# A diffusion block on one core: the first modulation as four column strips, one ring of weights, another layout for the merge

## The chip, the cores and the metric

The kernel runs on one core of a Trainium2 chip. The metric is device time in microseconds (us) of one execution. The kernel before took 1096.97 us, the median of three runs from 1096.02 to 1098.99. Engines are named as in the profile: PE is TensorE (PEld its weight loads), DVE VectorE, ACT ScalarE, POOL GpSimd, SP SyncE, which here only issues transfers.

## The reference

One layer of a diffusion transformer works on 512 latent tokens and 256 context tokens of width 1024, in float32. What matters for the change:

```
m_lat = (silu(c) @ mod_w + mod_b)            # six sections of 1024: sh1, sc1, g1, sh2, sc2, g2
m_ctx = silu(c_ctx) @ mod_w + mod_b
h_lat = rms_norm(x, g) * (1 + sc1) + sh1
h_ctx = rms_norm(ctx, g) * (1 + csc1) + csh1
... h @ w_in -> two token mixers (gated DeltaNet, HGRN2), gates g_a, g_b, m_a, m_b
ya = gated_head_norm(oa, g_a) @ w_up_a ;  yb = gated_head_norm(ob, g_b) @ w_up_b
x = x + g1 * ((sigmoid(m_a) * ya + sigmoid(m_b) * yb) @ w_out)
x = x + g2 * swiglu(rms_norm(x, g') * (1 + sc2) + sh2)
```

So the first two sections of `mod_w` (1024 by 2048 numbers) are needed for two vectors, the latent one and the context one, before the first projection can begin.

## The kernel before

Every large product is made in three parts of reduced-precision float32 (fp32r): each operand is split into a high part, `hi`, and the rest, `lo`, and hi·hi, hi·lo and lo·hi are summed in PSUM (`mm3`, L105). `split` (L92 to L97) loads a tile of weights on SP's queue, makes `hi` on ACT and `lo` on DVE; its buffers, two of each kind, are a ring named `ring["w"]`. All tiles are taken from pools that lie on top of each other in SBUF; a tile that comes to lie on an older one waits for that one's last use. The order of the instructions on each engine is set by a list scheduler from the order of the program and a priority, `tc.cur_priority`; stages of the two mixers are interleaved by the written plan `PLAN`.

The first stage runs so. `load_x` loads the tokens, `load_mod(d)` for each of eight blocks d of 128 output columns a tile `mw` with all 1024 rows of `mod_w` for a shift and a scale block, `wr` the raw weights of six gates. `modulation(d, s)` (L264, L266, L270) multiplies, on DVE, each of the eight 128-row parts of `mw` by its 128 numbers of the vector s (0 latent, 1 context) and adds them up in two accumulators `macc`; then PE sums over the partitions by four matmuls with a column of ones into `pmod0`. `mod_columns` (L275 to L277) adds the biases and multiplies by the norm's weights; the result, `mcol`, has a column for each feature block. `normed` transposes the tokens of block d on PE (L283, `px`), applies `mcol` twice on ACT (`hhi` L285 or `chi` for the context, and a float32 twin L287), and takes the low part on DVE (L288). `prepare(d)` does that for the latent tokens and splits `wr`. The loop over d then issues 18 matmuls (L316, `pg`) into six banks, after which two more gates (`gate`, `pgate`) are computed. Between them the context's eight modulations are issued, behind them the context's `normed`, and then the small projection `pab` (L369), with `abT` (L370), on which the DeltaNet's gates depend. The main stage follows: HGRN heads (`h_...`) and DeltaNet pairs (`g_...`, `p_...`), with gates in the gaps and further sections of the modulation on DVE (`mwe`, `mwb`; L111 sums their columns on four strips of the array, `column_sums`).

Late in that stage the first pool of the left side, `wp`, belongs to the stack `early` and is given up with it; a second ring, `wf`, was opened on the right side (after L911) and serves the remaining gates and everything behind them: the merge (`branch`, `up`, matmuls `pup`), the output projection (`pwo`) and the SwiGLU (`pf`, `pfo`). The merge's pool `mg` (its outputs `mh`, `ml`) lies below `yp` (the gated branch outputs `yh`, `yl`, the gates read back `ug`, `mg`, the branch outputs `uy`, and the product `us`).

Of the kernel before, what the change touches and what calls it, by code (L numbers as in the profile page):

```python
# [7 lines left out]
F32 = mybir.dt.float32  # L8
# [40 lines left out]
def body(tc, T, out, tap=None):  # L49
# [8 lines left out]
    with ExitStack() as root:  # L58
        def pool(name, bufs=1, side=None, **kw):
            return tc.tile_pool(name=name, bufs=bufs, side=side, reuse_waits="tile", **kw)  # L60

        cp = root.enter_context(pool("cp"))
        hpool = root.enter_context(pool("hpool"))
        early = ExitStack()
        ring = {"w": early.enter_context(pool("wp", 2))}
# [13 lines left out]
        def pmm(name):  # L79
            return bank("mm", name)  # L80
# [73 lines left out]
        with ExitStack() as st:  # L154
# [32 lines left out]
            def load_mod(d):  # L187
                mw = s1.tile([P, KT, 256], F32, name=f"mw{d}")
                for j in range(2):
                    nc.sync.dma_start(mw[:, :, P * j:P * j + P],  # L190
                                      T["mod_w"][0, :, D * j + P * d:D * j + P * d + P].rearrange("(k p) f -> p k f", p=P))
                mws.append(mw)

            load_mod(0)
            for g in (2, 3, 4, 5):
                load_x(g)
            for d in range(KT):
                if d > 0:
                    load_mod(d)
                wr = s1.tile([P, NG0 * P], F32, name=f"wr{d}", tag="wr", bufs=3)  # L200
                nc.sync.dma_start(wr[:, :], W_IN[P * d:P * d + P, C_MB:C_MB + NG0 * P])
                wraws.append(wr)
# [39 lines left out]

            ss = s1.tile([P, 6], F32, name="ss")
# [14 lines left out]
            def modulation(d, s):  # L258

                accs = [sp.tile([P, 256], F32, name=f"macc{d}_{s}{i}", tag=f"macc{i}", bufs=4) for i in range(2)]  # L260
                for k in range(KT):
                    acc, col = accs[k % 2], sc[:, 8 * s + k:8 * s + k + 1]
                    if k < 2:
                        nc.vector.tensor_scalar_mul(acc[:, :], mws[d][:, k, :], col)  # L264
                    else:
                        nc.vector.scalar_tensor_tensor(acc[:, :], mws[d][:, k, :], col, acc[:, :], op0=ALU.mult, op1=ALU.add)  # L266
                for j in range(2):
                    c = 16 * s + 2 * d + j
                    for i, acc in enumerate(accs):
                        nc.tensor.matmul(pmod0[:, c:c + 1], acc[:, P * j:P * j + P], ones[:, 0:1], start=(i == 0), stop=(i == 1))  # L270

            def mod_columns(s, d0, d1):

                ps = pmod0[:, 16 * s + 2 * d0:16 * s + 2 * d1].rearrange("p (d j) -> p d j", j=2)
                nc.vector.tensor_tensor(mcol[:, s, d0:d1, 0], ps[:, :, 0], mb_sh[:, d0:d1], op=ALU.add)  # L275
                nc.vector.tensor_tensor(mcol[:, s, d0:d1, 1], ps[:, :, 1], mb1[:, d0:d1], op=ALU.add)
                nc.vector.tensor_tensor(mcol[:, s, d0:d1, 1], mcol[:, s, d0:d1, 1], g_mix[:, d0:d1], op=ALU.mult)  # L277
# [13 lines left out]
            pmod0 = bank("ha", "pmod0")  # L291
# [11 lines left out]
            modulation(0, 0)  # L303
            mod_columns(0, 0, 1)
            prepare(0)
            modulation(1, 0)
            for d in range(KT):
                if d + 2 < KT:
                    modulation(d + 2, 0)
                if d + 1 < KT:  # L310
                    mod_columns(0, d + 1, d + 2)
                    prepare(d + 1)
                wh, wl = wparts[d]
                for n, (u, v) in enumerate(((wh, hhi), (wl, hhi), (wh, hlo))):
                    for i in range(NG0):
                        nc.tensor.matmul(pg0[i][:, :], u[:, P * i:P * i + P], v[:, d, :],  # L316
                                         start=(d == 0 and n == 0), stop=(d == KT - 1 and n == 2))
            for i in range(NG0):
                gate_out(16 + i, pg0[i], sp, "gt")
            norm_rows((0, 1))  # L320
            cd = list(range(KT))
# [5 lines left out]
            for d in cd:  # L327
                modulation(d, 1)
            mod_columns(1, 0, KT)
# [584 lines left out]
        wf = root.enter_context(pool("wf", 2, side="right"))  # L914
# [7 lines left out]
        ring["mod"] = md.enter_context(pool("md", side="right"))  # L922
        mods += [mod_quarter(*q) for q in quarters]
        here = tc.cur_priority
        tc.cur_priority = here + 5000
        while gates or mods:
            if gates:
                gate(gates.pop(0), ring["mod"], wf, "ga")
            mod_steps(6)
# [5 lines left out]
        early.close()  # L935
        tc.cur_priority = here + 5000 + 10000
        ring["w"] = wf

        with pool("mg", 1) as mg:
            mh = mg.tile([P, KT, SEQ], F32R, name="mh")  # L940
            ml = mg.tile([P, KT, SEQ], F32R, name="ml")
            mt = view(x1, 0, ((SEQ, KT), (1, SEQ)))
            with pool("yp", 1) as yp:
                def branch(br):

                    yh = yp.tile([P, NH, SEQ], F32R, name=f"yh{br}", tag="yh", bufs=2)
                    yl = yp.tile([P, NH, SEQ], F32R, name=f"yl{br}", tag="yl", bufs=2)
                    for h in range(NH):
                        gt = yp.tile([P, SEQ], F32, name=f"ug{br}{h}", tag="ug", bufs=4)
                        nc.sync.dma_start(gt[:, :], gdram[4 * br + h, :, :])  # L950
                        sg = yp.tile([P, SEQ], F32, name=f"us{br}{h}", tag="us", bufs=2)
                        nc.scalar.activation(gt[:, :], gt[:, :], AF.Silu)
                        yt = yp.tile([P, SEQ], F32, name=f"uy{br}{h}", tag="uy", bufs=3)
                        nc.sync.dma_start(yt[:, :], ydram[4 * br + h, :, :])
                        nc.vector.tensor_tensor(sg[:, :], gt[:, :], yt[:, :], op=ALU.mult)
                        nc.scalar.copy(yh[:, h, :], sg[:, :])
                        nc.vector.tensor_tensor(yl[:, h, :], sg[:, :], yh[:, h, :].bitcast(F32), op=ALU.subtract)
                    return yh, yl

                def up(br, W, ys):  # L960

                    for j in range(0, KT, 2):
                        w = split([W[:, P * j:P * j + 2 * P]], 4, 2 * P)
                        for i in (j, j + 1):
                            ps = pmm(f"pup{br}{i}")
                            o = P * (i - j)
                            mm3(ps[:, :], [lambda k, t=t: t[:, k, o:o + P] for t in w], [lambda k, t=t: t[:, k, :] for t in ys], 4)
                            gt = yp.tile([P, SEQ], F32, name=f"mg{br}{i}", tag="ug", bufs=4)
                            nc.sync.dma_start(gt[:, :], gdram[8 + 8 * br + i, :, :])
                            nc.scalar.activation(gt[:, :], gt[:, :], AF.Sigmoid)  # L970
                            if br == 0:
                                nc.vector.tensor_tensor(mt[:, i, :], gt[:, :], ps[:, :], op=ALU.mult)
                            else:
                                nc.vector.tensor_tensor(gt[:, :], gt[:, :], ps[:, :], op=ALU.mult)
                                nc.vector.tensor_tensor(gt[:, :], mt[:, i, :], gt[:, :], op=ALU.add)
                                nc.scalar.copy(mh[:, i, :], gt[:, :])
                                nc.vector.tensor_tensor(ml[:, i, :], gt[:, :], mh[:, i, :].bitcast(F32), op=ALU.subtract)
                        yield

                merge_a = up(0, T["w_up_a"][0], branch(0))  # L980
                next(merge_a)
                yb = branch(1)
                for _ in merge_a:
                    pass
                mod_sums()
                md.close()
                row_bcast(g1b, mbc[:, 16:24], "ga")
                nc.vector.scalar_tensor_tensor(A2[:, :], mbc[:, 32:40], 1.0, g_ffn, op0=ALU.add, op1=ALU.mult)
                for _ in up(1, T["w_up_b"][0], yb):
                    pass  # L990
# [134 lines left out]
```

## Time and profile before

| what | number |
|---|---|
| median of three runs | 1096.97 us |
| profiled execution, its own time | 1099.97 us |
| its span in the profile | 1098.3 us |
| mean granted clock of PE | 0.983 |
| PE busy | 1034.3 us, 94% |
| DVE busy | 699.2 us, 64% |
| ACT busy | 554.6 us, 50% |
| bytes moved | 122.06 MB, mean 111 GB/s |

The span runs from the first instruction to the last; some 1.7 us of the execution's own time lie outside it. PE counts as busy while a matmul is in its pipeline, and neighbours overlap, so the pace of matmuls is read from the chain (time of a group divided by its count), not from the mean duration of one.

### The profile page before, as it was taken

The numbers are of one execution on the slowest core, as the hardware profiler recorded it, in microseconds if no ns is written. First come the engines' busy times: TensorE is split into PE (matmuls) and PEld (weight loads), VectorE is DVE, ScalarE is ACT, GpSimd is POOL, SyncE is SP. The second block draws the span as 40 slices with busy tenths as digits, with TensorE's granted clock in tenths as the row PEclk, the third lists the DMA queues.
The fourth block names the chain that finished last, engine by engine and source line by source line (L and its number), as shares of the span: only waits on it lengthen the run. The fifth ranks groups of instructions, "written<-read, shape, count | busy, mean of one in ns | idle before, by whom it ended". The sixth has DMA issues, their size and how long they took to land.

```text
span 1098.3 us, 16604 instructions
## 1 busy us (share of the span) xinstructions
PE 1034.3 (94%) x6439; PEld 856.0 (78%) x6439; DVE 699.2 (64%) x1373; ACT 554.6 (50%) x1042; POOL 75.7 (7%) x132
## 2 busy tenths in 40 slices
PE   4999999979899999999989999999999999999996
PEld 3787788858797877789777787788888878888785
DVE  5896876789867967976796575686433333322524
ACT  3454578757877765887764743442222222221212
POOL 0010000220002022001111000110000000000000
PEclk9998999999999999999999999999999999999998
DMA  9943412122004213200728843454333323322222
GB/s 304 283 145 126 135 44 72 51 76 67 3 10 143 61 48 87 58 3 28 221 90 269 275 152 127 129 170 152 96 96 97 96 77 96 96 96 95 84 92 94
DMA packets 142721, 122.06 MB, mean 111 GB/s; under 512 B 5533, under 2 KB 118451, under 8 KB 142643
## 3 DMA queue, kind: packets, MB, share of 16 engines
q1 hardware_dynamic: 135907, 100.20, 30.0%
q0 software_dynamic: 4640, 17.30, 4.7%
q10 hardware_dynamic: 2096, 3.50, 0.9%
q8 instruction: 50, 0.82, 0.3%
q14 instruction: 28, 0.23, 0.1%
HBM read 110.51 MB, written 10.49 MB: 110 GB/s over the span
## 4 chain that ended last, share of the span: by engine, by line
PE 70%; DVE 12%; ACT 6%; issue 5%; DMA 4%; POOL 3%; SPq 0%; POOLq 0%; ACTq 0%; DVEq 0%
PE pf L105 22%; PE pfo L105 10%; PE pgate L105 5%; PE pup L105 4%; PE pg L316 3%; PE h_z L105 3%; PE pwo L105 3%; DVE lo L97 2%; PE h_zv L105 2%; PE p_s_pk L795 1%; PE pmod L270 1%; PE h_pA L482 1%; PE g_k_zl L105 1%; PE p_s_pk L786 1%; DMA mwb<-in_mod_w_dram 1%
## 5 line engine op out<-in xcount | busy, mean ns | idle before, releaser
L95 ACT CAST hi<-raw 128x1024 fp32r<-128x1024 f32 (+1 forms) x137 | 135.8, 992 | 310.1 <-PE pf L105 169.9
L97 DVE TENSOR_TENSOR lo<-raw,hi 128x1024 fp32r<-128x1024 f32 (+1 forms) x137 | 157.8, 1152 | 183.3 <-ACT hi L95 183.0
L105 PE MATMUL pf<-hhi,lo 128*128 128x512 f32 (+1 forms) x368 | 142.8, 389 | 0.4 <-DVE lo L97 0.4
L105 PE MATMUL pf<-hlo,hi 128*128 128x512 f32 (+1 forms) x368 | 142.8, 389 | 0.3 <-DVE hlo L1038 0.3
L105 PE MATMUL pf<-hhi,hi 128*128 128x512 f32 (+1 forms) x368 | 142.4, 389 | 0.0
L105 PEld LDWEIGHTS pf<-hhi,lo 128*128 128x128 f32 x368 | 70.2, 191 | 16.0 <-DVE lo L97 1.2
L105 PEld LDWEIGHTS pf<-hlo,hi 128*128 128x128 f32 x368 | 70.1, 191 | 15.3 <-DVE hlo L1038 0.5
L105 PEld LDWEIGHTS pf<-hhi,hi 128*128 128x128 f32 x368 | 69.9, 191 | 14.7
L105 PE MATMUL pfo<-lo,uh 128*128 128x512 f32 x176 | 69.8, 396 | 0.1
L105 PE MATMUL pfo<-hi,ul 128*128 128x512 f32 x176 | 69.5, 395 | 0.0
L105 PE MATMUL pfo<-hi,uh 128*128 128x512 f32 x176 | 68.7, 395 | 0.0
L105 PE MATMUL pgate<-hhi,lo 128*128 128x512 f32 x144 | 61.0, 424 | 6.2 <-DVE lo L97 6.2
L105 PE MATMUL pgate<-hhi,hi 128*128 128x512 f32 x144 | 60.5, 420 | 1.9 <-ACT hi L95 1.9
L105 PE MATMUL pgate<-hlo,hi 128*128 128x512 f32 x144 | 59.4, 413 | 0.0
L1061 DVE TENSOR_TENSOR sg<-sg,pf 128x512 f32<-128x512 f32 x22 | 15.1, 687 | 51.6 <-PE pf L105 51.5
L829 DVE SCALAR_TENSOR_TENSOR acc<-mwb,sc,acc 128x256 f32<-128x256 f32 x72 | 34.4, 482 | 10.1 <-DMA mwb<-in_mod_w_dram 8.9
L266 DVE SCALAR_TENSOR_TENSOR macc<-mw,sc,macc 128x256 f32<-128x256 f32 x96 | 39.9, 476 | 0.0
L105 PEld LDWEIGHTS pfo<-lo,uh 128*128 128x128 f32 x176 | 33.2, 188 | 8.6 <-DVE lo L97 1.0
L105 PEld LDWEIGHTS pgate<-hhi,lo 128*128 128x128 f32 x144 | 28.8, 200 | 13.8 <-DVE lo L97 8.6
L105 PEld LDWEIGHTS pfo<-hi,uh 128*128 128x128 f32 x176 | 32.9, 188 | 8.0 <-ACT hi L95 0.6
L105 PEld LDWEIGHTS pfo<-hi,ul 128*128 128x128 f32 x176 | 33.2, 188 | 7.6
L105 PE MATMUL h_z<-hhi,hi 128*128 128x512 f32 x96 | 38.1, 397 | 0.4 <-ACT abT L370 0.3
(426 smaller groups left out, 2523.0 us busy)
## 6 DMA issues: line engine op xcount, KB each, us to landing
raw<-in_ffn_w_in_dram SPq DMA_DIRECT2D x44, 512.0 KB, 3.8
raw<-in_w_in_dram SPq DMA_DIRECT2D x37, 512.0 KB, 3.9
raw<-in_ffn_w_out_dram SPq DMA_DIRECT2D x22, 512.0 KB, 3.5
mwb<-in_mod_w_dram POOLq DMA_DIRECT2D x18, 512.0 KB, 4.6
mw<-in_mod_w_dram SPq DMA_DIRECT2D x16, 512.0 KB, 6.2
mwe<-in_mod_w_dram POOLq DMA_DIRECT2D x7, 1024.0 KB, 6.2
gdram<-gt SPq DMA_DIRECT2D x24, 256.0 KB, 2.1
raw<-in_w_in_dram SPq DMA_DIRECT2D x18, 256.0 KB, 3.2
```

Of the source, the lines that this page charges most:

```text
L95: nc.scalar.copy(hi[:, :, :], raw[:, :, :])
L97: nc.vector.tensor_tensor(lo[:, :, :], raw[:, :, :], hi.bitcast(F32), op=ALU.subtract)
L105: nc.tensor.matmul(ps, a[u](k), b[v](k), start=(start and n == 0), stop=(stop and n == tot - 1))
L266: nc.vector.scalar_tensor_tensor(acc[:, :], mws[d][:, k, :], col, acc[:, :], op0=ALU.mult, op1=ALU.add)
L270: nc.tensor.matmul(pmod0[:, c:c + 1], acc[:, P * j:P * j + P], ones[:, 0:1], start=(i == 0), stop=(i == 1))
L316: nc.tensor.matmul(pg0[i][:, :], u[:, P * i:P * i + P], v[:, d, :], start=(d == 0 and n == 0), stop=(d == KT - 1 and n == 2))
L482: nc.tensor.matmul(pA[:, P * c:P * c + P], kq[:, 0, P * c:P * c + P], kq[:, 1, P * c:P * c + P], start=True, stop=True)
L786: nc.tensor.matmul(pk[:, P:2 * P], N[:, d, e, g, :], rt[:, :], start=True, stop=True)
L795: nc.tensor.matmul(pk[:, 2 * P:3 * P], kend[:, :], u[:, :], start=True, stop=True)
L829: nc.vector.scalar_tensor_tensor(acc[:, :], mw[:, k - k0, :], sc[:, k:k + 1], acc[:, :], op0=ALU.mult, op1=ALU.add)
L1061: nc.vector.tensor_tensor(sg[:, :], sg[:, :], pgu[1][:, :], op=ALU.mult)
```

## The change

Three things change.

First, the modulation. `load_mod(c)` now loads a tile of 512 rows (half of the inputs) by 512 columns (256 of the shift and 256 of the scale); six buffers serve eight such tiles, and the raw weights `wr` have five buffers instead of three. The latent tokens are loaded ahead of the first such tile. `modulation(q)`, called four times instead of sixteen, does two blocks d and both vectors at once: eight float32 matmuls, for each half of the rows one in each of the four 32-column strips of the array, with a 32-column operand `sch` that holds the two vectors and 30 columns of zeros, and 512 columns of `mod_w` streaming; each strip leaves its part of the sum on 32 partitions of one bank. DVE copies the bank to `mr`, and four matmuls with the two-column tile `comb` add the four strips and turn the result into columns; three DVE operations finish `mcol` for latent and context together. The DVE accumulation and the context's modulations between the gates are gone, and the context's row norms are issued inside the loop, at d = 6.

Second, `wp` now belongs to the root and is the ring for all stages; the gates of the late main stage get a ring of their own, `wx`, given up at the end of that stage. `wf` is gone.

Third, the merge's pools change places: `yp` is opened ahead of `mg`, its `yh`, `yl` are plain tiles, one for each branch, and the product is written into `yt` instead of a tile `sg`.

```
-            def load_mod(d):
-                mw = s1.tile([P, KT, 256], F32, name=f"mw{d}")
+            def load_mod(c):
+                mw = s1.tile([P, 4, 512], F32, name=f"mw{c}", tag="mw", bufs=6)
...
+            def modulation(q):
+                ps = bank("ha", f"pmod{q}")
+                for half in range(2):
+                    for k in range(4):
+                        nc.tensor.matmul(ps[32 * k:32 * k + 32, :], sch[:, 4 * half + k, :], mws[2 * q + half][:, k, :],
+                                         start=(half == 0), stop=(half == 1), tile_position=(0, 32 * k))
+                mr = s1.tile([P, 512], F32, name=f"mr{q}", tag="mr", bufs=2)
+                nc.vector.tensor_copy(mr[:, :], ps[:, :])
+                for i in range(4):
+                    nc.tensor.matmul(ps[:, 2 * i:2 * i + 2], mr[:, P * i:P * i + P], comb[:, :], start=True, stop=True)
...
-            modulation(0, 0)
-            mod_columns(0, 0, 1)
+            modulation(0)
             prepare(0)
-            modulation(1, 0)
             for d in range(KT):
-                if d + 2 < KT:
-                    modulation(d + 2, 0)
+                if d % 2 == 0 and d + 2 < KT:
+                    modulation(d // 2 + 1)
                 if d + 1 < KT:
-                    mod_columns(0, d + 1, d + 2)
                     prepare(d + 1)
+                if d == 6:
+                    norm_rows((0, 1))
...
             for i in rest[0:2]:
                 gate(i, sp)
-                for _ in range(8):
-                    if cd:
-                        modulation(cd.pop(0), 1)
...
-        wf = root.enter_context(pool("wf", 2, side="right"))
...
+        wx = gx.enter_context(pool("wx", 2, side="right"))
...
-        ring["w"] = wf
-        with pool("mg", 1) as mg:
+        with pool("yp", 1) as yp, pool("mg", 1) as mg:
...
-                        nc.vector.tensor_tensor(sg[:, :], gt[:, :], yt[:, :], op=ALU.mult)
+                    nc.vector.tensor_tensor(yt[:, :], gt[:, :], yt[:, :], op=ALU.mult)
```

More of the change, by code (lines that the diff above doesn't have):

```diff
@@ L63, in body @@
         hpool = root.enter_context(pool("hpool"))
+        ring = {"w": root.enter_context(pool("wp", 2))}
         early = ExitStack()
-        ring = {"w": early.enter_context(pool("wp", 2))}
         cpool = early.enter_context(pool("cpool"))
@@ L197, in body @@
             for d in range(KT):
[L198 to L202, printed above, removed]
+                load_mod(d)
+                if d % 2 == 0:
+                    continue
+                for e in (d - 1, d):
+                    wr = s1.tile([P, NG0 * P], F32, name=f"wr{e}", tag="wr", bufs=5)
+                    nc.sync.dma_start(wr[:, :], W_IN[P * e:P * e + P, C_MB:C_MB + NG0 * P])
+                    wraws.append(wr)
                 if d == 1:
@@ L241, in body @@
             nc.vector.tensor_scalar_add(mb1[:, :], mb_sc, 1.0)
+            sch = s1.tile([P, KT, 32], F32, name="sch")
+            nc.gpsimd.memset(sch[:, :, :], 0.0)
+            nc.vector.tensor_copy(sch[:, :, 0:2], sc.rearrange("p (s k) -> p k s", s=2))
+            comb = s1.tile([P, 2], F32, name="comb")
+            nc.vector.tensor_tensor(comb[:, :], ident[:, 0:2], ident[:, 32:34], op=ALU.add)
+            for j in (64, 96):
+                nc.vector.tensor_tensor(comb[:, :], comb[:, :], ident[:, j:j + 2], op=ALU.add)
             ss = s1.tile([P, 6], F32, name="ss")
@@ L256, in body @@
             mcol = s1.tile([P, 2, 8, 2], F32, name="mcol")
[L258 to L277, printed above, removed]
+            def modulation(q):
[8 more added lines that the diff above has]
+                    nc.tensor.matmul(ps[:, 2 * i:2 * i + 2], mr[:, P * i:P * i + P], comb[:, :], start=True, stop=True)
+                col = ps[:, 0:8].rearrange("p (j d s) -> p j s d", j=2, s=2)
+                dd = slice(2 * q, 2 * q + 2)
+                def both(x):
+                    return x[:, dd].unsqueeze(1).to_broadcast([P, 2, 2])
+                nc.vector.tensor_tensor(mcol[:, :, dd, 0], col[:, 0, :, :], both(mb_sh), op=ALU.add)
+                nc.vector.tensor_tensor(mcol[:, :, dd, 1], col[:, 1, :, :], both(mb1), op=ALU.add)
+                nc.vector.tensor_tensor(mcol[:, :, dd, 1], mcol[:, :, dd, 1], both(g_mix), op=ALU.mult)
@@ L290, in body @@
             norm_rows((2, 3, 4, 5))
-            pmod0 = bank("ha", "pmod0")
             pg0 = [bank(t, f"pg0_{i}") for i, t in enumerate(("mm", "mm", "ga", "ga", "ga", "fa"))]
@@ L319, in body @@
                 gate_out(16 + i, pg0[i], sp, "gt")
-            norm_rows((0, 1))
-            cd = list(range(KT))
             for i in rest[0:2]:
                 gate(i, sp)
-                for _ in range(8):
-                    if cd:
-                        modulation(cd.pop(0), 1)
-            for d in cd:
-                modulation(d, 1)
-            mod_columns(1, 0, KT)
             for d in range(KT):
@@ L922, in body @@
         ring["mod"] = md.enter_context(pool("md", side="right"))
+        gx = ExitStack()
+        wx = gx.enter_context(pool("wx", 2, side="right"))
         mods += [mod_quarter(*q) for q in quarters]
@@ L927, in body @@
             if gates:
-                gate(gates.pop(0), ring["mod"], wf, "ga")
+                gate(gates.pop(0), ring["mod"], wx, "ga")
             mod_steps(6)
@@ L940, in body @@
             mh = mg.tile([P, KT, SEQ], F32R, name="mh")
             ml = mg.tile([P, KT, SEQ], F32R, name="ml")
[L942 to L954, printed above, removed]
-                        nc.vector.tensor_tensor(sg[:, :], gt[:, :], yt[:, :], op=ALU.mult)
[L956 to L990, printed above, removed]
@@ L993, in body @@
+            merge_a = up(0, T["w_up_a"][0], branch(0))
+            next(merge_a)
+            yb = branch(1)
+            for _ in merge_a:
+                pass
+            mod_sums()
+            md.close()
+            row_bcast(g1b, mbc[:, 16:24], "ga")
+            nc.vector.scalar_tensor_tensor(A2[:, :], mbc[:, 32:40], 1.0, g_ffn, op0=ALU.add, op1=ALU.mult)
+            for _ in up(1, T["w_up_b"][0], yb):
+                pass
             with pool("xp", 2) as xp:
```

38 lines of the change are left out of this document (35 added, 3 removed).

## The prediction

> **What bounds the kernel now.** I read the page first, for the engine that fills the span.
>
> ```profile
> PE 1034.3 (94%) x6439; PEld 856.0 (78%) x6439; DVE 699.2 (64%) x1373; ACT 554.6 (50%) x1042; POOL 75.7 (7%) x132
> ...
> PE   4999999979899999999989999999999999999996
> ...
> DVE  5896876789867967976796575686433333322524
> ```
>
> TensorE (PE) is the bound almost everywhere, and VectorE (DVE) is close to it only in the first tenth. So a gain must take matmul time away, or a place where PE stands still. Next comes the chain that ended last, from the first projection matmul to the first dense stretch of the main stage.
>
> ```profile
> 19.68 1.65 PE pg L316 x3
> ...
> 60.36 7.74 PE pg L316 x34
> 68.11 5.45 PE pgate L105 x24
> 73.55 3.46 PE pmod L270 x32
> ...
> 77.59 0.54 PE px L283 x4
> ...
> 85.95 3.29 PE pmod L270 x24
> ...
> 90.82 0.57 ACT chi L285
> ...
> 97.64 1.87 PE pab L369 x10
> ...
> 99.53 0.58 ACT abT L370
> ...
> 101.78 1.35 PE h_z L105 x5
> ```
>
> Three parts are seen: the lat projection (pg) to 68.1; two gates, with the context's modulation between and behind them, to 91.4; the small a/b projection (pab) to 101.8, where the h_z matmuls of the first HGRN head become dense. Busy time of each engine in these parts, and in two late ones (DVE's, ACT's and POOL's columns follow PE's; then granted clock, DMA share, GB/s):
>
> ```profile
> 20.00:40.00 20.00, 18.16 (x83) 14.60 (x83) 16.45 (x44) 5.57 (x8) 0.00 (x0) 0.91 1.13 310
> ...
> 19.60:68.10 48.50, 46.58 (x229) 38.76 (x230) 41.82 (x114) 22.85 (x33) 1.38 (x2) 0.96 0.81 224
> 68.10:91.40 23.30, 21.13 (x120) 18.43 (x118) 20.58 (x57) 7.04 (x11) 1.94 (x2) 0.85 0.68 226
> 91.40:101.70 10.30, 9.95 (x53) 6.59 (x53) 5.04 (x16) 8.04 (x19) 0.32 (x6) 0.83 0.36 102
> 550.00:600.00 50.00, 45.25 (x243) 37.03 (x244) 40.31 (x76) 27.33 (x53) 6.53 (x8) 0.97 0.53 170
> 600.00:650.00 50.00, 49.22 (x293) 39.44 (x292) 32.03 (x48) 30.79 (x45) 0.00 (x0) 1.00 0.70 232
> ```
>
> Between 68.1 and 91.4 DVE is busy 20.6 of 23.3 us, and PE's granted clock is only 0.85: PE's "busy" there is partly slow and partly tiny matmuls that wait for DVE. What DVE does is the second half of these groups:
>
> ```profile
> L266 DVE SCALAR_TENSOR_TENSOR macc<-mw,sc,macc 128x256 f32<-128x256 f32 x96 | 39.9, 476 | 0.0
> L270 PE MATMUL pmod<-ones,macc 128*128 128x1 f32 x128 | 17.2, 252 | 6.0 <-DVE macc L266 6.0
> ...
> L264 DVE TENSOR_SCALAR macc<-mw,sc 128x256 f32<-128x256 f32 x32 | 9.9, 345 | 1.6 <-DMA mw<-in_mod_w_dram 1.6
> ```
>
> That is 49.8 us of DVE for the modulation of latent and context, one after the other.
>
> **The change part by part.**
>
> *Prices.* The code makes 64 pmod matmuls and L270 has 128 records, so a float32 matmul is two records. In the chain above, 32 records take 3.46 us, 0.108 us each. A gate matmul takes 5.45/24 = 0.227 us, a pg matmul 7.74/34 = 0.228, a px transpose 0.54/4 = 0.135. Further rows, from the chain and the timeline:
>
> ```profile
> 572.01 0.67 PE h_pS L548 x6
> ...
> 633.55 0.23 PE pmo L111 x16
> ```
> ```profile
> 289.09 0.92 PE L760 MATMUL p_pYb<-p_N,p_T 64*64 64x64 f32 x24 [0.34 <-ACT p_T L757]
> ```
>
> A float32 record that streams 128 columns takes 0.67/6 = 0.112 us, so one of 512 columns is four times that by estimate, 0.447 us. One strip modulation has 8 such matmuls, 16 records: 7.15 us one after another, 1.8 us if the four strips run side by side. Which of the two is the question of this case; the trace has no 512-column strip. Two rows are near. L111 works on the same four strips of 128 rows by 32 columns, and its 16 records need 0.23 us, 14 ns each, where the same matmul on the full array (pmod) needs 108. L760 runs two 64x64 corners of the array with 64 columns: alone a record would take 0.112/2 = 0.056 us, 24 of them 1.34 us, and they took 0.92. So parts of the array do run side by side. I take 1.8 us, because L111 has the same strips; 7.15 stays the other end. The four column matmuls behind them are 8 records of the pmod kind, 0.87 us. One modulation is then 2.7 us (4.4 two at a time: 3.6 + 0.87; 8.0 in a row).
>
> The page "TensorE: Matmul & The Clock Gate" of the Trainium skill (Part 3) gives 2.38 times for three column strips with 512 columns; by that share four strips would take about 1.8/0.79 = 2.3 us by estimate, and the sum below would be about 1.6 us worse. No run here shows a strip with a long moving operand.
>
> *Start.* The latent rows are now loaded before the modulation's weights, and the first modulation needs two weight tiles instead of one.
>
> ```profile
> 6.01 7.23 DMA xt<-in_x_dram
> ```
>
> The last x tile lands at 13.24 us with one 1.05 MB weight tile ahead of it; with one more, at 310 GB/s, the last of these loads lands 3.4 us later, at 16.6. Then: second half of the strips 0.9, a copy out of PSUM, 0.87 for the column matmuls, three small DVE operations, the first hhi.
>
> ```profile
> L1061 DVE TENSOR_TENSOR sg<-sg,pf 128x512 f32<-128x512 f32 x22 | 15.1, 687 | 51.6 <-PE pf L105 51.5
> ```
> ```profile
> 12.74 0.16 DVE L275 TENSOR_TENSOR mcol<-pmod,vc 128x1 f32<-128x1 f32 x1 [1.50 <-PE pmod L270]
> ...
> 13.68 0.16 DVE L277 TENSOR_TENSOR mcol<-mcol,vc 128x1 f32<-128x1 f32 x1
> ...
> 18.85 0.78 ACT L285 ACTIVATE hhi<-px,mcol 128x512 fp32r<-128x512 f32 x1 [3.65 <-PE px L283]
> ```
>
> The copy by L1061 0.69, the three operations 13.84 - 12.74 = 1.1, hhi 0.78: 16.6 + 0.9 + 0.69 + 0.87 + 1.1 + 0.78 = 20.9, and some 0.8 for handing over and a slow clock on the first strips: 21.7 against 19.68. **+2.0 us.** The memset of the padded weights on POOL, its copy and the three adds for the combining columns need only the constants and lie under the load.
>
> *Lat projection.* Taken off PE: seven of the eight latent modulations (the first lies before 19.68), 7 x 8 records x 0.108 = 6.0 us. Added: three strip modulations, 3 x 2.7 = 8.1. **+2.0 us.** DVE loses its accumulation, so what it keeps (wl, hlo, a copy) is hidden. The new wait is PE's, for mw tiles. Behind it stand the pg matmuls queued later. Tiles two and three land 2 x 0.39 + 2.1 MB later than 16.6, at 25.9 us; their modulation is needed for the third d, two d's of 18 matmuls after 21.7, at about 30. Put ahead of the first pg matmuls it would cost up to 4 us; put behind, nothing. I take nothing. SP's loads of the seventh weight tile wait for modulation 0 (about 20 us), before SP gets there. Two losses go:
>
> ```profile
> 27.35 1.22 PE L270 MATMUL pmod<-ones,macc 128*128 128x1 f32 x8 [0.29 <-DVE macc L266]
> 30.11 1.22 PE L316 MATMUL pg<-hhi,wh 128*128 128x512 f32 x2 [1.54 <-ACT hhi L285]
> ```
>
> PE stands 1.54 us before 30.11, because the second hhi waits for its modulation, which now comes with the first. **-1.5 us.** A mean clock of 0.96 over 48.5 us is at most 1.9 us lost; half goes with the DVE waits. **-1.0 us.**
>
> *Between 68.1 and 91.4.* The strips carry both vectors, so the context's modulation is gone. What stays on PE is 48 gate matmuls x 0.227 = 10.9 us and the 16 context transposes x 0.135 = 2.2: 13.1 of 23.3 us. **-10.2 us.** Late next is ACT:
>
> ```profile
> L285 ACT ACTIVATE chi<-px,mcol 128x256 fp32r<-128x256 f32 x8 | 4.5, 568 | 4.2 <-DVE mcol L277 3.9 <-PE px L283 0.3
> ```
>
> Chi and its float32 twin are 16 x 0.57 = 9.1 us of ACT, beside the copies of eight gates; that fits into 13 us only just, so I give back **+1.0 us.**
>
> *pab.* It now waits for chi one by one (ACT, 0.57 us twice for each d). With chi made during the gates it is PE's own work: 16 matmuls x 0.227 and 16 of half the length, 5.5 us, abT 0.58, and 0.9 from 100.89 to 101.78 for the small transposes: 7.0 of 10.3. **-3.3 us.**
>
> *Late part.* The low ring, the yp pool below mg and one product tile less change no instruction but the place of the product (into yt). The rows there:
>
> ```profile
> 587.35 11.63 PE pgate L105 x45
> ...
> 607.52 7.07 DMA raw<-in_w_up_a_dram
> ...
> 616.98 16.57 PE pup L105 x70
> ```
>
> The loads of w_up_a, the gates read back and the splits are covered by PE's own remaining gate matmuls: 49.22 of 50 us busy from 600 to 650. So earlier weights buy nothing there. If the cover went, the 7.07 us load would show. **0**, bounded by the idle 4.75 + 0.78 = 5.5 us of the two late windows as a gain and some 2 us of order on SP as a loss.
>
> Sum: 2.0 + 2.0 - 1.5 - 1.0 - 10.2 + 1.0 - 3.3 = **-11.0 us**. The profiled execution took 1099.97 us with a span of 1098.3; by it the change gives a span of 1087.3. The median of the runs is 1096.97, so the time is 1086.0.
>
> **The rivals.**
>
> *Strips in a row.* The four strips use all 128 rows, and each streams its own 512 columns; if PE takes one at a time, each later modulation costs 8.0 instead of 2.7 us and the first second half 3.6 instead of 0.9: 3 x 5.3 + 2.7 = 18.6. That ends at -11.0 + 18.6 = +7.6, 1104.6 us, **slower**. It decides from about 10 of these 18.6 us, where the gain is gone within the noise. For it: L111 streams only one column, so it proves overlapping loads more than overlapping streams. Against it: L760, which streams. The same page of the Trainium skill (Part 3) says that a weight load overlaps a running matmul only when the row group differs, which would put strips of equal rows in a row. The trace disagrees for plain matmuls: a gate matmul of 0.227 us with its load of the same 128 rows is paced as if the load cost nothing. Chance 0.08.
>
> *Two at a time*, as L760 shows it surely: 3 x 1.8 + 0.9 = 6.3 us more than the forecast, 1092.3. A stall of PE for mw tiles (4 us) ends near there too. Chance 0.10.
>
> *The front's gain is lost later.* From 100 to 600 us the order of two GDN pairs and four HGRN heads is set by PE, DVE and ACT together; if another engine's chain ends there last, it takes the 11 us back: 1096 to 1098. Against it: PE is busy nine tenths there, and its work only starts earlier. Chance 0.12.
>
> *The late part gains too.* The merge's weights no longer share a ring with the low gates, and the idle 5.5 us are filled: 1080.5. For it: 4.75 us idle at 550 to 600. Against it: these are waits of HGRN's own chain, short and in PE's queue order. Chance 0.10.
>
> **How the numbers follow.** The forecast has 0.60, its own range is 1082 to 1090 (the start, the clock and ACT's 1 us). The range from 1078 to 1098 takes in all but the first rival and some tails, about 0.85. About 0.3%, 3.3 us, is what a measurement of this kernel can tell from no change. Faster by more: forecast, late gain and most of two at a time, 0.78; within it: most of the lost gain and the rest of two at a time, 0.11; slower: strips in a row 0.08 and 0.03 of the lost gain, 0.11.
>
> **What would show it.** Right: 16 strip records in about 1.8 us and no macc group on DVE; the first pg near 21.7; pg's end near 69.5; dense h_z near 91 instead of 101.8; clock near 1.0 between; pup about 11 us earlier than 616.98. Wrong: strip records 0.4 us apart; pg's end past 75; PE waiting for mw; or the front at 91 and pup still after 612, which would be the lost gain.

## The result and the profile after

The changed kernel took 1089.15 us (median of five runs, 1083.01 to 1090.2), the kernel before 1098.59 beside it (1096.02 to 1099.42). The ratio is 0.9899, with a 95% interval of 0.9879 to 0.9919: faster by 1.0%. The profiled execution took 1089.27 us, its span is 1087.5 us. The prediction had 1086.0 and a span of 1087.3. The sum came out almost to the digit, and its terms did not: this is what the rest is about. In the tables below a median is over all runs, a few far slower ones among them (of no_ring's ten, one of 1260.94 and one of 1945.1 us), while ratio and interval are of the fast runs alone.

The page of the kernel after, first its engines, then VectorE's digits and the granted clock in 40 slices:

```profile
PE 1017.4 (94%) x6407; PEld 839.9 (77%) x6407; DVE 656.6 (60%) x1238; ACT 553.8 (51%) x1042; POOL 76.5 (7%) x133
...
DVE  3337886789767958976796665587343433422524
...
PEclk9999999989999999999999999999999999999999
```

VectorE's first three digits have gone from 5, 8, 9 to 3, 3, 3: the accumulation is gone. PE has lost 17 us of busy time, more than the front can explain. The timeline of PE at the start (start, time, then what; in brackets the idle time before it and what ended it):

```profile
13.14 1.93 PE L274 MATMUL pmod<-mw,sch 128*32 128x512 f32 x8 [7.39 <-DVE xt L265]
...
16.11 1.94 PE L274 MATMUL pmod<-mw,sch 128*32 128x512 f32 x8 [0.21 <-DMA mw<-in_mod_w_dram]
...
18.85 1.05 PE L279 MATMUL pmod<-comb,mr 128*128 128x2 f32 x8 [0.40 <-DVE mr L277]
22.04 2.93 PE L325 MATMUL pg<-hhi,wh 128*128 128x512 f32 x6 [2.13 <-ACT hhi L296]
...
27.38 1.07 PE L274 MATMUL pmod<-mw,sch 128*32 128x512 f32 x8
28.38 0.66 PE L294 MATMUL px<-sq,xt 128*128 128x128 f32 x4
```

Each line of L274 is one half of a strip modulation, four matmuls of two records. The first two take 1.93 and 1.94 us; the granted clock up to 22 us is given as 1.00 (first row of the windows below), so it does not tell why. From the third on, eight records take 1.06 to 1.07 us, where one after another they would take 8 x 0.447 = 3.6 by estimate. The four strips run side by side. The first pg matmul starts at 22.04.

The windows that follow (us, then busy time of PE, PEld, DVE, ACT and POOL, clock, DMA share, GB/s):

```profile
0.00:22.00 22.00, 6.51 (x29) 2.29 (x29) 7.94 (x27) 8.44 (x14) 3.18 (x9) 1.00 0.94 320
...
22.00:70.00 48.00, 47.56 (x244) 33.97 (x245) 16.70 (x31) 21.46 (x31) 3.55 (x8) 0.97 0.74 241
70.00:82.00 12.00, 11.89 (x56) 9.67 (x54) 2.52 (x3) 5.40 (x9) 0.00 (x0) 1.00 0.79 233
82.00:92.00 10.00, 7.13 (x41) 3.88 (x41) 4.80 (x13) 8.85 (x20) 0.00 (x0) 1.00 0.51 161
...
600.00:650.00 50.00, 45.85 (x280) 36.71 (x279) 30.53 (x48) 28.15 (x41) 0.00 (x0) 1.00 0.62 200
```

From 70 to 92 the clock is 1.00, where the like stretch had 0.85; from 22 to 70 it is 0.97, where it was 0.96. From 82 to 92 PE is idle for 2.9 us of 10 while ACT is busy 8.85. And in the merge, where PE had been busy 49.22 of 50 us, it is now busy 45.85: waits that were not there before. The h_z matmuls become dense at 93.97, where they did at 101.78:

```profile
92.46 0.39 PE L105 MATMUL h_z<-hhi,hi 128*128 128x512 f32 x1
...
93.97 0.50 PE L105 MATMUL h_z<-hhi,lo 128*128 128x512 f32 x1
```

Then the tail. The chain that ended last (start, time, group and its count), of the kernel before:

```profile
726.25 167.37 PE pf L105 x718
...
966.09 58.57 PE pfo L105 x252
1028.60 55.24 PE pfo L105 x236
```

and of the kernel after:

```profile
752.85 135.63 PE pf L105 x597
...
957.98 57.30 PE pfo L105 x252
1019.11 54.01 PE pfo L105 x236
```

These are the same matmuls on the same engine at the same granted clock: 1.00 in both traces from 720 to 893 us and from 900 us to the last pfo. The last 236 of the output of the SwiGLU took 234.1 ns each (55.24/236) and now take 228.9; the 252 before them went from 232.4 to 227.4 ns, the pf matmuls from 233.1 (167.37/718) to 227.2 (135.63/597). Nothing in the change touches these lines. From the first start of pf to the last of pfo it was 380.85 us (708.16 to 1089.01) and is 372.54 (705.61 to 1078.15). So 8.3 of the 10.8 us of span come from a stage that the prediction left alone.

The first start of some tiles in the traces, in us, shows where the rest lies; the columns to the right belong to experiments below:

| tile | before | after | mod_only | before_pad | high_pad | best2 |
|---|---|---|---|---|---|---|
| first pg | 19.68 | 22.04 | 21.66 | 19.97 | 22.00 | 21.57 |
| first h_z | 100.16 | 92.46 | 93.95 | 99.00 | 94.51 | 90.17 |
| first pup (merge) | 610.19 | 605.53 | 605.33 | 607.86 | 604.11 | 596.00 |
| last pup | 659.09 | 657.30 | 654.31 | 654.82 | 652.04 | 642.97 |
| first pf | 708.16 | 705.61 | 703.50 | 703.08 | 700.32 | 691.23 |
| last pfo | 1089.01 | 1078.15 | 1083.02 | 1075.35 | 1072.68 | 1066.53 |

The front's gain is 7.7 us at the first h_z, 4.7 at the merge's start, 1.8 at its end. Single traces of one and the same front differ by up to three microseconds (with the new front the first h_z comes at 91.81 in ring_below and at 94.80 in no_ring), so small differences in this table carry nothing. Averages are safer. In the five traces with the old front (before, ring_only, lay_only, before_pad, low_shift) the first h_z comes at 100.1 and the first pup at 610.8; in the seven with the new one (after, mod_only, no_ring, ring_below, high_pad, raw_high, offset_scan) at 93.3 and 605.2. By them the front gains 6.8 us, and 5.6 of these reach the merge.

### The profile page after: what moved, and what is told of

Read it like the earlier page. It is cut to its first block, busy times and chain, and to the rows that moved or that the text cites. A ratio compares the mean times of both kernels' runs of the same rounds, so it can differ in the third digit from the quotient of the medians.

```text
span 1087.5 us, 16405 instructions
## 1 busy us (share of the span) xinstructions
PE 1017.4 (94%) x6407; PEld 839.9 (77%) x6407; DVE 656.6 (60%) x1238; ACT 553.8 (51%) x1042; POOL 76.5 (7%) x133
## 4 chain that ended last, share of the span: by engine, by line
PE 51%; DVE 9%; issue 8%; DMA 5%; ACT 4%; POOL 2%; SPq 0%; POOLq 0%; DVEq 0%; ACTq 0%
PE pf L105 18%; PE pfo L105 10%; PE pwo L105 3%; PE pup L105 3%; DMA mwb<-in_mod_w_dram 3%; PE pgate L105 2%; DVE lo L97 2%; PE h_z L105 2%; PE h_zv L105 2%; PE h_pA L483 1%; PE p_s_pk L796 1%; PE p_s_pk L787 1%; PE p_s_pk L784 1%; DVE p_o L689 1%; DVE p_Z L691 1%
## 5 line engine op out<-in xcount | busy, mean ns | idle before, releaser
L105 PE MATMUL pf<-hhi,lo 128*128 128x512 f32 (+1 forms) x368 | 140.0, 381 | 2.0 <-DVE lo L97 2.0
L105 PE MATMUL pf<-hlo,hi 128*128 128x512 f32 (+1 forms) x368 | 140.1, 382 | 0.7 <-DVE hlo L1039 0.7
L105 PE MATMUL pf<-hhi,hi 128*128 128x512 f32 (+1 forms) x368 | 139.6, 382 | 0.0
L1062 DVE TENSOR_TENSOR sg<-sg,pf 128x512 f32<-128x512 f32 x22 | 15.1, 687 | 49.0 <-PE pf L105 48.9
L105 PE MATMUL h_z<-hhi,lo 128*128 128x512 f32 x96 | 38.1, 396 | 0.0
```

What stands on the lines that cost most here:

```text
L105: nc.tensor.matmul(ps, a[u](k), b[v](k), start=(start and n == 0), stop=(stop and n == tot - 1))
L1062: nc.vector.tensor_tensor(sg[:, :], sg[:, :], pgu[1][:, :], op=ALU.mult)
```

## The experiments

**First: one part at a time.** Three kernels make one part of the change alone on the kernel before, the fourth leaves one part out. My theory was that the modulation makes the gain. A rival was that one of the two layouts does.

*mod_only*: the strip modulation alone, both rings and the merge as before.

```
+            def modulation(q): ...          # the first part of the change, whole
         wf = root.enter_context(pool("wf", 2, side="right"))     # kept
```

> The kernel before with the strip modulation alone. Theory 1 (the front pays, as predicted): about 11 us below before, 1087. Theory 2 (the front's gain melts away by the merge, and the late gain of the changed kernel comes from another matmul pace): the h_z matmuls begin some 8 us early, the merge's end is only about 2 us early, matmuls of 512 columns in the SwiGLU keep 232 ns, and the time is 1 to 4 us below before, 1094 to 1097.

*ring_only*: the low ring alone.

```
-        ring = {"w": early.enter_context(pool("wp", 2))}
+        ring = {"w": root.enter_context(pool("wp", 2))}
...
-        wf = root.enter_context(pool("wf", 2, side="right"))
+        wx = gx.enter_context(pool("wx", 2, side="right"))
```

> The kernel before with the one low ring alone (the late gates in a ring of their own). Theory 1: no change, within 2 us of before. Theory 2a (the pace hangs on where the late ring lies): matmuls of 512 columns from the merge on go from 232 to 227 ns each, about 2000 of them, so about 10 us below before, 1087 to 1089. Theory 2b (the pace is the state of a run or of a chip, not of the kernel): 232 or 227 in this kernel and in before alike.

*lay_only*: the third part of the change alone: the merge's pools in the new order, plain tiles `yh` and `yl`, the product in `yt`.

```
-        with pool("mg", 1) as mg:
+        with pool("yp", 1) as yp, pool("mg", 1) as mg:
```

> The kernel before with the merge's pools in their new places alone, late ring on the right as before. Theories 1 and 2a: no change, pace 232 ns, within 2 us of before. If the pace hangs on where the merge's or the SwiGLU's other tiles lie: 227 ns from the merge on only as far as those tiles are used.

*no_ring*: the kernel after with the late ring back on the right.

```
+        wf = root.enter_context(pool("wf", 2, side="right"))
...
-        wx = gx.enter_context(pool("wx", 2, side="right"))
+        ring["w"] = wf
```

> The changed kernel with the late ring put back on the right side, the rest as changed. Theory 1: as the changed kernel, 1086 to 1089. Theory 2a: pace 232 ns again from the merge on, about 10 us slower than the changed kernel, 1095 to 1099.

Measured, beside 1099.34 us of the kernel before on the same chip; the last column is the time of the last 236 pfo matmuls from the chain of waits:

| kernel | median us | ratio | 95% interval | pfo x236, us |
|---|---|---|---|---|
| mod_only | 1093.98 | 0.9959 | 0.9935 to 0.9983 | 55.23 |
| ring_only | 1104.11 | 1.0047 | 1.0019 to 1.0074 | 54.02 |
| lay_only | 1101.52 | 1.0011 | 0.9992 to 1.0030 | 55.23 |
| no_ring | 1098.73 | 0.9975 | 0.9950 to 0.9999 | 55.42 |

The modulation alone brings 0.4%, by the ratio some 4.5 us (1.9 to 7.1 by its interval) and not 11. The low ring alone is slower, though its tail has the fast pace: its merge takes 58.7 us from the first to the last pup, where the kernel before takes 48.9. The fast pace goes with the ring, and the ring costs time in the merge. In the groups by line (busy and mean ns, then the idle time before and what ended it), the merge of the kernel before:

```profile
L105 PE MATMUL pup<-yh,hi 128*128 128x512 f32 x64 | 25.4, 397 | 0.3 <-DVE vc L856 0.3
```

of ring_only:

```profile
L105 PE MATMUL pup<-yh,hi 128*128 128x512 f32 x64 | 28.6, 453 | 7.4 <-ACT yh L957 4.2 <-DVE x L973 3.1 <-DVE vc L856 0.2
```

and of the kernel after:

```profile
L105 PE MATMUL pup<-yh,hi 128*128 128x512 f32 x64 | 25.2, 394 | 3.8 <-DVE x L971 3.5 <-DVE vc L857 0.3
```

With the low ring PE waits for the split branch output (4.2 us) and for the product with the gate (3.1). With the new order of the pools the first of these waits is gone, and the second stays at 3.5 us. Two rows of the waits of the kernel after stand near it:

```profile
ACT mg L969 <- DMA mg<-gdram: 10.3, 9, 3.0
...
DVE x L971 <- PE pup L105: 5.3, 4, 2.0
```

and one of ring_only:

```profile
ACT mg L971 <- DMA mg<-gdram: 6.4, 8, 1.5
```

ACT waits 10.3 us, nine times, for the gates read back; before it was 6.4 us in six times. But in ring_only it waits no longer than before, 6.4 us, and PE waits 3.1 us for the product all the same, so late gates cannot be all of it. The third part of the change repairs most of what the second breaks, and does nothing measurable by itself (lay_only). What makes PE wait for the product, and why the gates come late in the kernel after, I did not test.

**Second: what the pace hangs on.** The late ring's split tiles lie on the right in the kernel before and low in the kernel after. Three kernels keep the ring on the right and shift it. The memory map of the compiled programs gives the starts in a partition: the latents `hhi` at byte 20576, the late ring's first `hi` at 212960 in the kernel before and in no_ring, at 53344 in the kernel after.

*ring_below*: no_ring with the x1 pool opened ahead of the ring, so that the ring lies 20 KB lower.

```
-        wf = root.enter_context(pool("wf", 2, side="right"))
         x1p = root.enter_context(pool("x1p", side="right"))
...
+        wf = root.enter_context(pool("wf", 2, side="right"))
```

> The changed kernel with the late ring on the right side again, but below the tile x1, so that its split weights lie from 188 to 204 KiB of a partition instead of from 208 to 224. Theory A (the pace hangs on a weight tile's place, and only the very top of SBUF is slow): 227 ns for a matmul of 512 columns in the SwiGLU; the merge takes 48 us as with the ring on the right, so 4 to 5 us below the changed kernel, 1083 to 1086. Theory B (any place on the right is slow): 232 ns and 1092 to 1097.

*high_pad*: no_ring with a tile of 896 bytes ahead of the ring; the region stays, the start moves.

```
+        padr = root.enter_context(pool("padr", side="right"))
+        nc.vector.memset(padr.tile([P, 224], F32, name="padt")[:, :], 0.0)
         wf = root.enter_context(pool("wf", 2, side="right"))
```

> The late ring at the top of the right side with 896 bytes of padding behind it: the same region, but the start of each tile has the same remainder by 1024 bytes as in the low ring. Theory C (the pace hangs on the alignment of a tile): 227 ns, 1083 to 1089. Theory A (on the region): 232 ns, 1092 to 1098.

*raw_high*: no_ring with the unsplit tiles (which the transfers fill) on the right in a pool of their own, and only the split ones, which PE reads, moved down.

```
+            rp = ring["raw"] if pool is ring.get("late") else pool
+            raw = rp.tile([P, kt, n], F32, name=f"raw{WN[0]}", tag="raw", bufs=2)
```

> As ring_below, but the raw weights, which transfers write and ACT and DVE read, lie at the top of SBUF (216 to 224 KiB), and the split weights, which PE reads, from 180 to 196 KiB. If it is PE's own reads of the top that are slow: 227 ns and 1083 to 1086. If it is the traffic of transfers, ACT and DVE into the top that slows PE: 232 ns and 1092 to 1097.

*best1* belongs to the front and is told with it below. Beside 1099.12 us of the kernel before; "distance" is the start of `hi` less the start of `hhi`, modulo 256 bytes:

| kernel | start of hi | distance | median us | ratio | 95% interval | pfo x236, us |
|---|---|---|---|---|---|---|
| no_ring (first call) | 212960 | 128 | 1098.73 | 0.9975 | 0.9950 to 0.9999 | 55.42 |
| ring_below | 192352 | 0 | 1087.17 | 0.9888 | 0.9861 to 0.9914 | 54.02 |
| high_pad | 212064 | 0 | 1084.58 | 0.9891 | 0.9851 to 0.9932 | 54.02 |
| raw_high | 184160 | 0 | 1088.04 | 0.9902 | 0.9881 to 0.9923 | 54.02 |

It is not the region (high_pad stays in it) and not the transfers into the unsplit tiles (raw_high leaves them on the right). It is the start of the tiles that PE reads. The distances are 0 modulo 256 and not modulo 512 in ring_below and raw_high (192352 - 20576 = 671 x 256, an odd multiple), so 256 is enough.

The same map settles two more points. The other operands of these matmuls (`yh`, `mh` and `uh` with their low parts) start at the same byte modulo 256 as `hhi`, so the distance holds for every 512-column matmul of the merge, the output projection and the SwiGLU, whichever of its two operands moves. And between no_ring and raw_high the late ring's `hi` and `lo` are the only tiles in SBUF whose start modulo 256 differs, so nothing else that was moved along can be the cause.

**Third: the pad alone, and start or distance.**

*before_pad*: the kernel before with the same pad of 896 bytes on the right. No part of the change is in it.

> The kernel before, and the only edit is one unused tile of 896 bytes a partition, opened on the right ahead of the late ring of weights: no modulation, no low ring, no new order of the merge's pools. It moves the late ring's split weights, the input tile (x1) and what follows them from starts at 224 of 256 bytes to starts at 96, where the widened matmuls of high_pad ran at 226.7 ns. Theory of the start addresses: the 512-column matmuls from 565 us on go from 232.4 to about 227 ns each, some 2,000 of them, so 10 to 11 us of the tail: 1,086 to 1,090 us, ratio 0.989 to 0.992, with the front unchanged (dense h_z near 100, first pup near 610) and the SwiGLU plus output projection 8 us shorter. Rival (the gain of the late stages is bound to the strip modulation or to where the low ring lies): no change, 1,097 to 1,099 us and 232 ns.

*low_shift*: the kernel before with 128 bytes ahead of `hhi`, so that `hhi` and the early ring move from 96 to 224 of 256 bytes. The late ring stays where it was, at 224.

```
+        padl = root.enter_context(pool("padl"))
+        nc.vector.memset(padl.tile([P, 32], F32, name="padt")[:, :], 0.0)
         hpool = root.enter_context(pool("hpool"))
```

> The kernel before, and the only edit is one unused tile of 128 bytes a partition at the low end, ahead of the normalised latents (hhi, hlo): they, and the early ring of weights above them, move from starts at 96 of 256 bytes to starts at 224; the late ring stays at 224. If the matmul's pace goes by the distance between the two operands' starts, modulo 256 bytes, all stages have distance 0: about 227 ns from 565 us on, and 1,086 to 1,090 us. If it goes by the absolute start of the weights, every 512-column matmul of both rings takes about 232.5 ns: the early stages lose what the late ones keep, so slower than before, by up to 5.7 ns on each wide matmul before 565 us (1,097 to 1,106 us). If by the absolute start of the moving operand alone, the same for all stages that read hhi. If neither, no change: 1,097 to 1,099 us.

*offset_scan*: no_ring with late split tiles that start at another multiple of 32 bytes for each pair of splits.

```
+                o = 8 * (WN[0] // 2 % 8)
+                hi, lo = [pool.tile([P, kt * n + 56], ...)[:, o:o + kt * n] ... for h in ("hi", "lo")]
```

> The kernel after with the late ring kept on the right as before, and each pair of split tiles there starts at another offset inside its buffer: 32 bytes times (number of the split / 2 mod 8), so that one trace holds the matmul's pace at eight starts modulo 256 bytes, on weights of the same stages. Theory: the pace is about 232 ns at 224 and 227 at 96; what it is at the six others is open. If only the sum modulo 64 or 128 counted, there would be two groups of equal starts; if a 128-byte half of 256 bytes counts, four starts are fast and four slow. Rival (no effect of the start): one pace for all eight. The time itself is of no weight here, near the middle between 1,084 and 1,099 us.

Measured, beside 1099.68 us of the kernel before: before_pad 1088.94 us, ratio 0.9896 (0.9875 to 0.9917); low_shift 1092.21 us, ratio 0.9932 (0.9911 to 0.9954); offset_scan 1094.11 us in its one run. The chain of before_pad:

```profile
750.00 135.67 PE pf L105 x597
...
1016.31 54.01 PE pfo L105 x236
```

of low_shift:

```profile
755.82 137.22 PE pf L107 x597
...
1025.29 53.99 PE pfo L107 x236
```

and of offset_scan:

```profile
749.09 140.45 PE pf L114 x598
...
1022.68 55.30 PE pfo L114 x236
```

One unused tile in the kernel before gives the whole of the change's gain: 0.9896 against 0.9899. Low_shift has the fast pace with both operands at 224 of 256 bytes, so it is not the start of one operand that counts, but the two starts against each other: distance 0 is fast, at 96 as at 224. Its early stages kept their pace too: pg and h_z matmuls that follow each other start 227 ns apart (median), as in the kernel before. The kernel before itself shows both paces: the gates of its first stage, whose weights lie in the early ring at distance 0, take 5.45/24 = 227 ns by the chain shown with the prediction, its last stages 232 to 234. Low_shift gains less in all than before_pad because it comes to the merge later (first pup at 612.32 us, 607.86 in before_pad); why, stays open.

The scan shows less than I had hoped. Its mean time from one wide matmul to the next is 230 to 234 ns at all eight distances, and 232 at distance 0. In it `hi` and `lo` of one weight never have the same start (their buffers differ by 64 bytes modulo 256), so each run of matmuls at distance 0 has neighbours that are not. Where two that follow each other are both at distance 0, they start 229.5 ns apart (76 pairs); where both are at 192 bytes, 229.0 (67 pairs); at the six other distances 231 to 235. So one aligned tile among others that are not brings little. Another distance is in the kernel before and the kernel after: 216 of their gates' matmuls have 64 bytes, and start 230 to 231 ns after the one before where nothing holds them up, beside 228 for the gates at 0 in the same traces. Which other distances would be fast stays open, and so does what in the chip makes the difference.

**Fourth: the front.** In the kernel after, the context is not normed during the gates. The program issues its norm behind them, and PE transposes the context from 80.92 us on, right behind the last gate matmul (80.69):

```profile
80.69 0.39 PE L105 MATMUL pgate<-hhi,lo 128*128 128x512 f32 x1
80.92 0.82 PE L294 MATMUL px<-sq,xt 128*128 128x128 f32 x6
```

The timeline of ACT shows the rest:

```profile
74.00 1.24 ACT L131 COPY gt<-pg 128x512 f32<-128x512 f32 x2 [2.71 <-DMA gdram<-gt]
...
78.25 1.20 ACT L131 COPY gt<-pg 128x512 f32<-128x512 f32 x2 [1.75 <-DMA gdram<-gt]
81.22 0.59 ACT L131 COPY gt<-pgate 128x512 f32<-128x512 f32 x1 [1.78 <-DMA gdram<-gt]
...
82.65 0.57 ACT L296 ACTIVATE chi<-px,mcol 128x256 fp32r<-128x256 f32 x1
84.37 0.58 ACT L131 COPY gt<-pgate 128x512 f32<-128x512 f32 x1 [1.15 <-DMA gdram<-gt]
```

The gate copies have two buffers, and a copy waits until the transfer of the one before the last is out: 7.4 us in four waits. The chi operations are issued behind these copies on ACT, and pab waits for chi. So chi is late for two reasons, the place of the context's norm behind the gates and the copies; the two kernels that follow change both at once and do not part them.

*best1*: ring_below with eight buffers for the gate copies, and the context normed ahead of the two gates.

```
-                gate_out(16 + i, pg0[i], sp, "gt")
+                gate_out(16 + i, pg0[i], sp, "gt", 8)
+            for d in range(KT):
+                normed(d, 1, (0, 1), chi, clo, "ha")
             for i in rest[0:2]:
-                gate(i, sp)
-            for d in range(KT):
-                normed(d, 1, (0, 1), chi, clo, "ga")
+                gate(i, sp, n=8)
```

> As ring_below, and in the first stage the gate copies have eight buffers instead of two and the context's transposes, from another pair of banks, stand before the two gates instead of behind them. Theory (chi is late because its ACT work stands behind gate copies that wait for their transfers): chi is made during the gates, pab no longer waits, the h_z matmuls become dense 3 to 6 us earlier (near 89), and the time is 3 to 6 us below ring_below. Rival (ACT's own work is the bound there, chi would be late anyway): within 2 us of ring_below.

Measured: 1089.62 us, ratio 0.9918 (0.9894 to 0.9941), no better than ring_below (0.9888). Chi is made from 73 to 81 us, as wanted, but now the split of the second gate's weights stands behind it on ACT. PE's timeline:

```profile
82.30 0.50 PE L105 MATMUL pgate<-hhi,hi 128*128 128x512 f32 x1 [2.81 <-ACT hi L95]
```

*best2*: high_pad with the same, and both gates' weights split ahead of the gate copies.

```
+            gws = [split([W_IN[:, gcols[i]:gcols[i] + P]], KT, P) for i in rest[0:2]]
             for i in range(NG0):
-                gate_out(16 + i, pg0[i], sp, "gt")
-            for i in rest[0:2]:
-                gate(i, sp)
+                gate_out(16 + i, pg0[i], sp, "gt", 8)
             for d in range(KT):
-                normed(d, 1, (0, 1), chi, clo, "ga")
+                normed(d, 1, (0, 1), chi, clo, "ha")
+            for i, w in zip(rest[0:2], gws):
+                gate_out(i, feat(w, lat, SEQ, f"pgate{i}"), sp, "gt", 8)
```

> high_pad (strip modulation, merge order of the change, late ring on the right behind a pad of 896 bytes) with the end of the front ordered anew: both gates' weights are split ahead of the gate copies, the context is normed right behind the six gate copies, in the bank that the modulation has left, and the gate copies have eight buffers, so that ACT waits for no write to DRAM. Theory: chi is ready before the gates end, and neither gate waits for its weights, so the projection of the context to the first dense phase takes about 8 us in place of 12.9: dense h_z near 89 in place of 94.5, and 2 to 4 us of it are left at the end: 1,080 to 1,083 us against 1,084.6 of high_pad. Rival (the front's gain melts by the merge, whose weights and loads are set by other queues): no change beside high_pad, 1,084 to 1,086 us.

Measured: 1078.82 us (1077.62 to 1081.66), ratio 0.9814 (0.9797 to 0.9831), against 0.9891 of high_pad: better than both kernels. Its timeline of ACT, and then its windows:

```profile
71.17 1.07 ACT L95 CAST hi<-raw 128x1024 fp32r<-128x1024 f32 x1
72.12 1.59 ACT L131 COPY gt<-pg 128x512 f32<-128x512 f32 x3
73.55 0.62 ACT L296 ACTIVATE chi<-px,mcol 128x256 fp32r<-128x256 f32 x1
```
```profile
70.00:82.00 12.00, 12.00 (x61) 9.30 (x60) 4.63 (x9) 12.00 (x25) 0.00 (x0) 1.00 0.77 256
82.00:92.00 10.00, 10.00 (x57) 6.53 (x55) 4.60 (x16) 3.36 (x8) 0.16 (x2) 1.00 0.56 169
```

No copy waits for a transfer, ACT is full from 70 to 82 us, and PE has no gap until the main stage, whose first h_z comes at 90.17 us instead of 94.51. I expected 2 to 4 us from that at the end; the table of starts gives 4.3 at h_z and 6.2 at the last pfo. The two us beyond the front are in no step that I worked out.

## Why the prediction was right in its sum and wrong in its parts

*The strips: right.* They run side by side, and both rivals that doubted it are out. The price was a little low: the next work starts 1.00 us after a half (27.38 to 28.38), so a modulation streams for 2.0 us and not 1.8. The share that the Trainium skill, page "TensorE: Matmul & The Clock Gate" (Part 3), gives for three strips had made it 2.3 by estimate; the trace lies between.

*Start, lat projection and the stall: right in sum.* First pg at 22.04 instead of 21.7, the end of pg at 70.03 instead of 69.5. The clock's term in it did not come: of the 1.0 us most is missing, for the mean clock of this stretch is 0.97 after 0.96. The stretch took 48.0 us as forecast all the same; what made up for it I did not work out.

*The give-back to ACT and pab: wrong in size.* The step that failed is "With chi made during the gates". I compared ACT's sum of work with the time and found that it fits; but the program issues the context's norm behind the gates, PE transposed the context only at 80.92, and ahead of chi on ACT stood copies that waited 7.4 us for transfers. From the end of pg to the dense h_z I had 21.5 us (69.5 to 91); it took 23.9 (70.03 to 93.97). That is 2.4 us of the term, and best2, whose first h_z comes 2.3 us before that of the kernel after, shows that they were there to be had.

*The front's gain kept to the end: right in part.* "Its work only starts earlier" held in the main stage for 4.7 of 7.7 us in this pair of traces, and for 5.6 of 6.8 in the averages above. Up to 0.8 us of the 4.7 is not the front's: 168 of the late gates' matmuls went from distance 128 to 0 as well (4 to 5 ns each). Where neither the low ring nor a new distance is in the way, 4.5 us (mod_only) and 2.7 us (no_ring) are left in the whole, by ratios whose intervals overlap. The rival of the lost gain had 0.12, and at the first pf it looks true: the kernel after is ahead by 2.55 us there, of which the faster pace of the 384 pup and pwo matmuls makes some 2 (384 x 5 to 6 ns). But the larger part of what is missing, some 4 us, went in the merge, and not in the stage from 100 to 600 us that the rival names.

*The late part: wrong.* The term of 0, with its bounds of 5.5 us as a gain and some 2 us as a loss, failed on both sides. The step that failed is "change no instruction but the place of the product": I took an instruction's time to be independent of where its operands lie. The 1920 matmuls with 512 columns of the merge, the output projection and the SwiGLU became 5.0 to 5.9 ns shorter each if all go as the chain's rows of pf and pfo do, 10 to 11 us; before_pad measures 11.4 (1.04% of 1099.68). And the merge, "covered by PE's own remaining gate matmuls", lost some 4: from the first pup to the first pf it took 97.97 us and takes 100.08, though the pace alone should have made it 2 us shorter.

So 11.0 us forecast and 10.8 us measured are two different sums: forecast as the gain of the front, measured as 8 us at the front, of which 4.7 reach the merge, 4 us lost in the merge, and 10 to 11 us from an alignment that nobody wrote into the diff. That the two sums agree is luck. What I named as marks of a right prediction would have told: the dense h_z came 3 us late, and pup started 5 us earlier and not 11.

## What to carry to other kernels

When a diff changes where tiles lie, compare the pace of the untouched matmuls first (time of a group in the chain, divided by its count); a run with nothing but a pad in the old kernel tells in one look what the layout alone is worth. Before giving work to an engine that "has time", read its queue, and that of the engine that feeds it, in program order: what stands ahead of the new work counts, not the sum of its busy time. And a sum that comes out right is no proof of its terms: test the parts alone.

## What the runs showed of the hardware

With 128-row float32 operands split as here, a matmul with 512 columns takes 227 to 229 ns in the chain when both operands start at the same byte modulo 256 in their partition, and 232 to 234 ns when they start 128 bytes apart: 54.0 against 55.2 to 55.4 us for 236 of them, in all kernels above that have one distance throughout these stages. The Trainium skill's page "SBUF — State Buffer" (section "Operand start alignment") asks only for a start at a multiple of the element size, speaks of legality and not of speed, and says that its runs timed nothing. By that rule all these starts are allowed; in speed they differ here.

Four 32-column strips with 512 columns each run beside one another: eight records in 1.07 us, where 3.6 us is the estimate for one after another.
